# Delta rule in a hybrid decoder step: two rooms for the inverse W, and squares written over tiles that are filled next

## The chip, the cores and the metric

The kernel runs on one core of a Trainium2 chip. The metric is device time of one execution in microseconds, median of several runs. A core has five engines with queues of their own: TensorE (PE, with its weight loads as PEld), VectorE (DVE), ScalarE (ACT), GpSimd (POOL) and SyncE (SP, which here only issues transfers). Each engine takes its own queue in order; between engines, semaphores order the work.

## What is computed

One layer of a decoder trunk on 1024 prompt rows and 8 sample rows of width 1024: a projection, a gated delta rule (8 heads of 128 x 128), sliding-window attention, a gated mix, and a convolutional feed-forward block. The change touches the delta rule on the prompt alone. In the reference:

```python
u = jnp.einsum('bhnij,bhnjv->bhniv', t_inv, v * beta[..., None])
w = jnp.einsum('bhnij,bhnjk->bhnik', t_inv, kb * jnp.exp(decay)[..., None])
...
def step(S, inp):
    u_n, w_n, a_n, qd_n, kd_n, last_n = inp
    v_new = u_n - jnp.einsum('bhck,bhkv->bhcv', w_n, S)
    o = jnp.einsum('bhck,bhkv->bhcv', qd_n, S) + jnp.einsum('bhij,bhjv->bhiv', a_n, v_new)
    S = S * last_n[..., None, None] + jnp.einsum('bhck,bhcv->bhkv', kd_n, v_new)
    return S, o
```

`t_inv` is the inverse of a unit triangular matrix per chunk; `q` and `k` are divided by their row norms, and the output `o` of each row by its root mean square.

## The kernel before

The kernel works in chunks of 128 rows, 8 chunks a head. Around the change, five streams run for each head h (loop at L1889):

- **prepare** (`delta_prepare`, for head h+1): loads the decay row into G (L854), masks it on POOL (L855), subtracts on DVE (L857), exponentiates on ACT (L858). It turns K and Q chunk by chunk on PE (tile `tp`), sums their squares on ACT (L870, the squares themselves go to a junk tile `osq`), makes `kd` on DVE (L872), then the products K K and K Q on PE (L888, L889), from which DVE makes A (L890) and U (L892, in the room of G). V is turned into `vn` (L900).
- **inverse** (`unit_inverse`, head h): inverts the triangular blocks U. 15 steps of a recurrence on DVE (L1001, L1002), round trips through DRAM (`ud`, `wd`), and then three doublings: PE products L1020 and L1026 (32 x 32 blocks), L1038 and L1043 (32 x 32 off the diagonal), L1052 and L1056 (64 x 64). Results go from PSUM into W by ACT: the four diagonal blocks (L1031), the off-diagonal 32 blocks (L1047), the last 64 x 64 block (L1057). L1045 copies a block to the tile `w01`, which DVE turns (L1049) for L1052; L1053 copies the product of L1052 for L1056.
- **scan** (`delta_scan`, head h): the chain over 8 chunks. For each chunk: PE L929 (K with the state S), DVE L930 (y), PE L932 (W with y), ACT L934 (s), PE L936 (kd with s), DVE L945 (new S); beside it PE L939 and L940 sum the output. After chunks 3 and 7 ACT squares the four outputs (L951, squares to a junk tile `osq2`, which shares its name `osq` in the profile), DVE and POOL make the factor f, DVE scales into `vn` (L958), and PE turns that (L189, `rc<-ident,vn`).
- **gate** (head h) and **projections** (K, Q, V of head h+2, or later gates): long rows of matmuls at L180 to L182, out of `mm3`. They depend on nothing in the chain. I call them projections below; they are what PE does while it waits for the chain.

No order is written by hand. Streams carry priorities (`weave`: start and step in the list at L1894 to L1904), and a scheduler sets each engine's queue before the run, from the priorities, from what each instruction needs, and from the rooms: a tile with `bufs=1` can only be written once all readers of its last user are done. W is one tile for all heads (L1884), so L1031 of head h stands behind the last L932 of head h-1. The scheduler's order is fixed when the program runs.

Of the kernel before, what the change touches and what calls it, by code (L numbers as in the profile page):

```python
# [12 lines left out]
AF = mybir.ActivationFunctionType  # L13
# [5 lines left out]
P = 128  # L19
# [5 lines left out]
NCH = 8  # L25
# [39 lines left out]
class Step:  # L65
# [782 lines left out]
    def delta_prepare(self, pool, psum, h):  # L848
        nc = self.nc
        K, Q, V = self.kqv[h]  # L850

        G = self.t(pool, [P, NCH, P], "G", bufs=1)
        rows = self.drow[h * NCH:(h + 1) * NCH]
        nc.sync.dma_start(G, rows[:, 0, :].unsqueeze(0).broadcast_to([P, NCH, P]))  # L854
        nc.gpsimd.affine_select(out=G, in_=G, pattern=[[0, NCH], [1, P]], compare_op=ALU.is_ge, fill=NEG,  # L855
                                base=0, channel_multiplier=-1)
        nc.vector.tensor_tensor(G, G, bc(self.d[:, h, :], 2, P), op=ALU.subtract)  # L857
        nc.scalar.activation(G, G, AF.Exp)  # L858


        kd = self.t(pool, [P, NCH, P], "kd", bufs=2)
        n2 = self.t(pool, [P, 2, NCH], "n2", bufs=2)
        for a, src in ((0, K), (1, Q)):
            for c0 in (0, 4):
                tp = self.t(psum, [P, 4, P], "tp", bufs=2)
                for c in range(4):
                    self.transpose(tp[:, c, :], src[:, c0 + c, :])
                junk = self.t(pool, [P, P], "osq", bufs=1)
                for c in range(4):
                    nc.scalar.activation(junk, tp[:, c, :], AF.Square, accum_out=n2[:, a, c0 + c:c0 + c + 1])  # L870
                if a == 0:
                    nc.vector.tensor_tensor(kd[:, c0:c0 + 4, :], tp, bc(self.edd[:, h, c0:c0 + 4], 2, P), op=ALU.mult)  # L872
                yield
        nc.vector.tensor_scalar_add(n2, n2, 4 * EPS)
        nk = self.t(pool, [P, NCH], "nk", bufs=2)
        self.power(nk, n2[:, 0, :], self.phalf)
        nc.vector.tensor_scalar_mul(nk, nk, 0.5)
        c1 = self.t(pool, [P, 2, NCH], "c1", bufs=2)
        nc.vector.reciprocal(c1[:, 1, :], n2[:, 0, :])
        nc.vector.tensor_tensor(c1[:, 0, :], c1[:, 1, :], self.beta[:, h, 0:8], op=ALU.mult)  # L880
        nc.vector.tensor_scalar_mul(c1[:, 1, :], c1[:, 0, :], -1.0)

        A = self.t(pool, [P, NCH, P], "A", bufs=2)
        U = G
        for c0 in range(0, NCH, 2):
            kk = self.t(psum, [P, 2, 2, P], "tp", bufs=2)
            for c in range(2):
                nc.tensor.matmul(kk[:, 0, c, :], K[:, c0 + c, :], K[:, c0 + c, :], start=True, stop=True)  # L888
                nc.tensor.matmul(kk[:, 1, c, :], K[:, c0 + c, :], Q[:, c0 + c, :], start=True, stop=True)  # L889
            nc.vector.tensor_tensor(A[:, c0:c0 + 2, :], kk[:, 1], G[:, c0:c0 + 2, :], op=ALU.mult)  # L890
            for c in range(2):
                nc.vector.scalar_tensor_tensor(U[:, c0 + c, :], kk[:, 0, c, :], c1[:, 1, c0 + c:c0 + c + 1],  # L892
                                               G[:, c0 + c, :], op0=ALU.mult, op1=ALU.mult)
            yield
        vn = self.t(pool, [P, NCH, P], "vn", bufs=2)
        for c0 in (0, 4):
            tp = self.t(psum, [P, 4, P], "tp", bufs=2)
            for c in range(4):
                self.transpose(tp[:, c, :], V[:, c0 + c, :])
            nc.vector.tensor_tensor(vn[:, c0:c0 + 4, :], tp, bc(nk[:, c0:c0 + 4], 2, P), op=ALU.mult)  # L900
            yield
        for c in (0, 4):
            e = self.t(pool, [P, 4, P], "ed", bufs=1)
            nc.sync.dma_start(e, rows[c:c + 4, 1, :].unsqueeze(0).broadcast_to([P, 4, P]))
            nc.vector.tensor_tensor(Q[:, c:c + 4, :], Q[:, c:c + 4, :], e, op=ALU.mult)
        self.prep = U, kd, A, vn, n2, c1

    def delta_scan(self, pool, psum, h, prep):
        nc, sg = self.nc, self.sg
        (K, Qd, _), W = self.kqv[h], self.W  # L910
        _, kd, A, vn, n2, c1 = prep
        S = None
        self.steps, self.at, self.every = [], 0, 2

        def step(ins):
            if h + 2 >= H:
                self.steps.append(ins.ins)

        so = self.t(pool, [P, NCH], "so", bufs=2)
        f = self.t(pool, [P, NCH], "f", bufs=2)  # L920
        for n in range(NCH):
            if n % 4 == 0:
                ops = self.t(psum, [P, 4, P], "o", bufs=1)
            if S is None:
                y = vn[:, n, :]
            else:
                y = self.t(pool, [P, P], "y", bufs=2)
                ks = self.t(psum, [P, P], "rc", bufs=2)
                yield step(nc.tensor.matmul(ks, K[:, n, :], S, start=True, stop=True))  # L929
                nc.vector.scalar_tensor_tensor(y, ks, self.ned[:, h, n:n + 1], vn[:, n, :], op0=ALU.mult, op1=ALU.add)  # L930
            sp = self.t(psum, [P, P], "rc", bufs=2)
            yield step(nc.tensor.matmul(sp, W[:, n, :], y, start=True, stop=True))  # L932
            s = self.t(pool, [P, P], "s", bufs=2)
            nc.scalar.activation(s, sp, AF.Copy, scale=c1[:, 0, n:n + 1])  # L934
            ds = self.t(psum, [P, P], "rc", bufs=2)
            yield step(nc.tensor.matmul(ds, kd[:, n, :], s, start=True, stop=True))  # L936
            o = ops[:, n % 4, :]
            if S is not None:
                nc.tensor.matmul(o, Qd[:, n, :], S, start=True, stop=False)  # L939
            nc.tensor.matmul(o, A[:, n, :], s, start=S is None, stop=True)  # L940
            S2 = self.t(pool, [P, P], "S", bufs=2)
            if S is None:
                nc.vector.tensor_copy(S2, ds)
            else:
                nc.vector.scalar_tensor_tensor(S2, S, self.edl[:, h, n:n + 1], ds, op0=ALU.mult, op1=ALU.add)  # L945
            S = S2
            if n % 4 == 3:
                c0 = n - 3
                junk = self.t(pool, [P, P], "osq2", bufs=1)
                for c in range(4):  # L950
                    nc.scalar.activation(junk, ops[:, c, :], AF.Square, accum_out=so[:, c0 + c:c0 + c + 1])  # L951

                nc.vector.tensor_scalar_mul(so[:, c0:c0 + 4], so[:, c0:c0 + 4], 1.0 / P)
                nc.vector.scalar_tensor_tensor(so[:, c0:c0 + 4], n2[:, 1, c0:c0 + 4], EPS * P, so[:, c0:c0 + 4],
                                               op0=ALU.mult, op1=ALU.add)
                self.power(f[:, c0:c0 + 4], so[:, c0:c0 + 4], self.mhalf)
                on = vn[:, c0:c0 + 4, :]
                nc.vector.tensor_tensor(on, ops, bc(f[:, c0:c0 + 4], 2, P), op=ALU.mult)  # L958
            if n in (5, NCH - 1):
                c0 = 4 if n == NCH - 1 else 0  # L960
                tp = self.t(psum, [P, 4, P], "rc", bufs=2)
                for c in range(4):
                    self.transpose(tp[:, c, :], vn[:, c0 + c, :])
                g = sg[:, c0 * P:(c0 + 4) * P]
                nc.vector.scalar_tensor_tensor(g, tp.rearrange("p c i -> p (c i)"), self.onw, g,
                                               op0=ALU.mult, op1=ALU.mult)

        queue = nc.sync if h + 1 < H else nc.gpsimd
        queue.dma_start(self.O[2][0, 0, h], S)
        queue.dma_start(self.oa[h][:, 0:NP], sg[:, 0:NP])  # L970

    def unit_inverse(self, pool, psum, h, U):

        nc, W = self.nc, self.W
        ud = self.t(self.dr, [NCH, 4, 32, 32], "ud", bufs=2)
        blocks = [slice(32 * b, 32 * b + 32) for b in range(4)]
        pairs = [(blocks[0], blocks[1]), (blocks[2], blocks[3])]
# [4 lines left out]
        for p in range(4):  # L982
            c = slice(16 * (p % 2), 16 * (p % 2) + 16)
# [57 lines left out]
        for n in range(NCH):  # L1041
            for a, b in pairs:
                nc.tensor.matmul(qp[a, n, :], Zc[b, n, :], W32[b, n, :], start=True, stop=True)  # L1043
        w01 = self.t(pool, [32, NCH, 32], "w01", bufs=1)
        nc.scalar.copy(w01, qp[0:32])  # L1045
        for a, b in pairs:
            nc.scalar.copy(W[a, :, b], qp[a])  # L1047
# [784 lines left out]
    def run(self):  # L1832
        S, nc = ExitStack, self.nc
        self.constants()
        with S() as ca:
# [45 lines left out]
            self.fill_where, self.gt = [self.fill_side], (pgt, "gt")  # L1881
            with S() as c:
                pa, pool, psum = self.pool("pa", 1, ctx=c), self.pool("p4", 1, ctx=c), self.pool("q4", 1, PSUM, ctx=c)
                self.W = self.t(pool, [P, NCH, P], "W", bufs=1)  # L1884
                nc.gpsimd.memset(self.W, 0.0)
                self.kqv = {}
                self.weave((self.delta_project(pa, pool, 0), 0, 1))
                self.weave((self.delta_prepare(pool, psum, 0), 0, 1), (self.delta_project(pa, pool, 1), 100, 1))
# [66 lines left out]
```

## Time and profile before

| | us |
|---|---|
| runs | 2159.11, 2160.53, 2164.14 |
| median | 2160.53 |
| the profiled execution's own time | 2164.56 |
| its span, first to last instruction | 2162.7 |
| PE busy | 2087.4 |
| DVE busy | 1334.1 |
| ACT busy | 815.5 |
| POOL busy | 314.2 |
| mean granted TensorE clock (share of full) | 0.977 |

The delta rule's heads run from about 430 to 1140 us of the span. A row of the timeline gives start, length, engine, line, tiles and count; in brackets, how long the engine had been idle before it and who ended that. A row of the windows gives for a stretch the busy time of each engine, then the granted clock (PEclk). A matmul's length includes the depth of the array, so two matmuls in a row start closer together than their lengths say; the distance of starts is what a matmul costs. A plain f32 matmul is two rows of the profile, so one L932 counts as x2.

### The profile page before, as it was taken

The numbers are of one execution on the slowest core, as the hardware profiler recorded it, in microseconds if no ns is written. First come the engines' busy times: TensorE is split into PE (matmuls) and PEld (weight loads), VectorE is DVE, ScalarE is ACT, GpSimd is POOL, SyncE is SP. The second block draws the span as 40 slices with busy tenths as digits, with TensorE's granted clock in tenths as the row PEclk, the third lists the DMA queues.
The fourth block names the chain that finished last, engine by engine and source line by source line (L and its number), as shares of the span: only waits on it lengthen the run. The fifth ranks groups of instructions, "written<-read, shape, count | busy, mean of one in ns | idle before, by whom it ended". The sixth has DMA issues, their size and how long they took to land.

```text
span 2162.7 us, 41246 instructions
## 1 busy us (share of the span) xinstructions
PE 2087.4 (97%) x16514; PEld 1975.9 (91%) x16514; DVE 1334.1 (62%) x2884; ACT 815.5 (38%) x2093; POOL 314.2 (15%) x434
## 2 busy tenths in 40 slices
PE   7999999999899999998999999999999999999998
PEld 4876877899899998998999999999999999999998
DVE  6656775474564765665324665478867767865565
ACT  5544554333334344334222532354434334421102
POOL 3000000120321111111111100003323323100000
PEclk9999998999999989999999999999999999999999
DMA  9434231241322222221328845323232232353202
GB/s 330 141 101 160 82 121 43 82 128 38 88 65 74 60 67 58 47 67 49 89 62 253 288 128 147 114 64 99 79 99 69 69 98 69 114 218 124 75 3 80
DMA packets 257946, 223.91 MB, mean 104 GB/s; under 512 B 57586, under 2 KB 224277, under 8 KB 257738
## 3 DMA queue, kind: packets, MB, share of 16 engines
q1 hardware_dynamic: 254714, 212.50, 32.1%
q0 software_dynamic: 1568, 4.95, 0.7%
q10 hardware_dynamic: 1472, 3.82, 0.5%
q8 instruction: 130, 2.13, 0.4%
q14 instruction: 62, 0.51, 0.1%
HBM read 171.25 MB, written 52.33 MB: 103 GB/s over the span
## 4 chain that ended last, share of the span: by engine, by line
PE 61%; DVE 5%; DMA 3%; ACT 2%; issue 1%; POOL 1%; SPq 1%; POOLq 0%; DVEq 0%; ACTq 0%
PE mm L180 14%; PE mm L181 14%; PE mm L182 14%; PE wv L181 3%; PE wv L180 3%; PE wv L182 3%; PE wy L182 2%; PE wy L180 2%; PE wy L181 2%; DMA b1l<-dlr 1%; PE tp L189 1%; DVE fa L1629 1%; DMA raw<-in_w_o_dram 1%; PE rc L932 1%; PE rc L936 1%
## 5 line engine op out<-in xcount | busy, mean ns | idle before, releaser
L180 PE MATMUL mm<-b1h,wh 128*128 128x384 f32 (+1 forms) x1440 | 472.8, 330 | 5.2 <-ACT gt L1265 1.9
L181 PE MATMUL mm<-b1l,wh 128*128 128x384 f32 (+1 forms) x1440 | 467.5, 325 | 0.9 <-DVE b1l L130 0.9
L182 PE MATMUL mm<-b1h,wl 128*128 128x384 f32 (+1 forms) x1440 | 467.7, 326 | 0.6 <-DVE wl L130 0.5
L180 PEld LDWEIGHTS mm<-b1h,wh 128*128 128x128 f32 x1440 | 273.0, 190 | 13.3 <-issue 4.7
L181 PEld LDWEIGHTS mm<-b1l,wh 128*128 128x128 f32 x1440 | 273.6, 190 | 5.7 <-issue 4.1
L182 PEld LDWEIGHTS mm<-b1h,wl 128*128 128x128 f32 x1440 | 272.9, 190 | 6.4 <-issue 4.3
L130 DVE TENSOR_TENSOR wl<-raw,wh 128x1024 fp32r<-128x1024 f32 x76 | 92.9, 1222 | 69.4 <-ACT wh L129 68.4
L129 ACT ACTIVATE wh<-raw 128x1024 fp32r<-128x1024 f32 x77 | 80.6, 1047 | 124.2 <-PE mm L181 89.6
L180 PE MATMUL mm<-pk,w 128*128 128x260 f32 (+1 forms) x440 | 124.4, 283 | 1.0 <-ACT pk L129 0.6
L181 PE MATMUL mm<-pk,w 128*128 128x260 f32 (+1 forms) x440 | 124.2, 282 | 0.8 <-DVE pk L130 0.8
L182 PE MATMUL mm<-pk,w 128*128 128x260 f32 (+1 forms) x440 | 124.1, 282 | 0.0
L180 PE MATMUL mm<-b2h,wh 128*128 128x384 f32 (+1 forms) x384 | 122.8, 320 | 1.2 <-ACT wh L129 1.2
L181 PE MATMUL mm<-b2l,wh 128*128 128x384 f32 (+1 forms) x384 | 121.9, 318 | 0.0
L182 PE MATMUL mm<-b2h,wl 128*128 128x384 f32 (+1 forms) x384 | 121.3, 318 | 0.0
L180 PE MATMUL mm<-bmh,pk 128*128 128x260 f32 (+1 forms) x380 | 109.4, 288 | 1.9 <-ACT pk L129 1.8
L182 PE MATMUL mm<-bmh,pk 128*128 128x256 f32 (+1 forms) x380 | 109.5, 288 | 1.1 <-DVE pk L130 1.1
L1418 DVE SCALAR_TENSOR_TENSOR x<-mm,mT,x 128x256 f32<-128x256 f32 (+2 forms) x133 | 63.6, 482 | 74.7 <-PE mm L182 70.8
L181 PE MATMUL mm<-bml,pk 128*128 128x260 f32 (+1 forms) x353 | 101.1, 286 | 0.0
L180 PE MATMUL mm<-bmh,w 128*128 128x260 f32 (+1 forms) x320 | 91.0, 284 | 0.0
L182 PE MATMUL mm<-bmh,w 128*128 128x260 f32 (+1 forms) x320 | 90.8, 284 | 0.0
L130 DVE TENSOR_TENSOR w<-ws,w 128x512 fp32r<-128x512 f32 x88 | 60.2, 686 | 41.5 <-ACT w L129 41.5
L180 PEld LDWEIGHTS mm<-pk,w 128*128 128x128 f32 x440 | 82.7, 188 | 1.6 <-ACT pk L129 0.8
(607 smaller groups left out, 5708.2 us busy)
## 6 DMA issues: line engine op xcount, KB each, us to landing
raw<-in_w_in_dram SPq DMA_DIRECT2D x60, 512.0 KB
bml<-act SPq DMA_DIRECT2D x22, 516.0 KB
raw<-in_w_ffn_gate_dram SPq DMA_DIRECT2D x22, 512.0 KB
raw<-in_w_ffn_up_dram SPq DMA_DIRECT2D x22, 512.0 KB
raw<-in_w_ffn_down_dram SPq DMA_DIRECT2D x22, 512.0 KB
qst<-in_w_mod_dram SPq DMA_DIRECT2D x16, 512.0 KB
raw<-in_w_mod_dram SPq DMA_DIRECT2D x16, 512.0 KB
act<-fa SPq DMA_DIRECT2D x22, 260.0 KB
```

What stands on the lines that cost most here:

```text
L129: self.nc.scalar.activation(hi, x, AF.Copy)
L130: (eng or self.nc.vector).tensor_tensor(lo, x, hi.bitcast(F32), op=ALU.subtract)
L180: mm(ps, whi, xhi, start=first, stop=False, **kw)
L181: mm(ps, whi, xlo, start=False, stop=False, **kw)
L182: self.last = mm(ps, wlo, xhi, start=False, stop=last, **kw)
L189: return self.nc.tensor.transpose(out, in_, self.ident[:p, :p])
L932: yield step(nc.tensor.matmul(sp, W[:, n, :], y, start=True, stop=True))
L936: yield step(nc.tensor.matmul(ds, kd[:, n, :], s, start=True, stop=True))
L1418: nc.vector.scalar_tensor_tensor(x[:, :np_], ps[:, :np_], self.mT[:, m + j, 8:9], x[:, :np_], op0=ALU.mult, op1=ALU.add)
L1629: nc.vector.scalar_tensor_tensor(ai[:, c:e], zi[:, j + c:j + e], col(j), ai[:, c:e], op0=ALU.mult, op1=ALU.add)
```

## The change

- W becomes a list of two tiles, and head h uses `W[h % 2]`. Both are cleared once at the start.
- The tile A of a head is taken before the squares, and L870 writes the squares of K, then of Q, into A, chunk by chunk; L890 overwrites them later. The tile `osq` is gone.
- L951 writes the squares of the outputs into `vn`, which L958 overwrites next. The tile `osq2` is gone.
- L1045 copies into the first 32 partitions of U16, whose last reader L1020 is done by then. The tile `w01` is gone.

```diff
         kd = self.t(pool, [P, NCH, P], "kd", bufs=2)
         n2 = self.t(pool, [P, 2, NCH], "n2", bufs=2)
+        A = self.t(pool, [P, NCH, P], "A", bufs=2)
...
-                junk = self.t(pool, [P, P], "osq", bufs=1)
                 for c in range(4):
-                    nc.scalar.activation(junk, tp[:, c, :], AF.Square, accum_out=n2[:, a, c0 + c:c0 + c + 1])
+                    nc.scalar.activation(A[:, c0 + c, :], tp[:, c, :], AF.Square, accum_out=n2[:, a, c0 + c:c0 + c + 1])
...
-        A = self.t(pool, [P, NCH, P], "A", bufs=2)
...
-        (K, Qd, _), W = self.kqv[h], self.W
+        (K, Qd, _), W = self.kqv[h], self.W[h % 2]
...
-                junk = self.t(pool, [P, P], "osq2", bufs=1)
                 for c in range(4):
-                    nc.scalar.activation(junk, ops[:, c, :], AF.Square, accum_out=so[:, c0 + c:c0 + c + 1])
+                    nc.scalar.activation(vn[:, c0 + c, :], ops[:, c, :], AF.Square, accum_out=so[:, c0 + c:c0 + c + 1])
...
-        nc, W = self.nc, self.W
+        nc, W = self.nc, self.W[h % 2]
...
-        w01 = self.t(pool, [32, NCH, 32], "w01", bufs=1)
+        w01 = U16[0:32]
...
-                self.W = self.t(pool, [P, NCH, P], "W", bufs=1)
-                nc.gpsimd.memset(self.W, 0.0)
+                self.W = [self.t(pool, [P, NCH, P], f"W{i}", bufs=1) for i in range(2)]
+                for w in self.W:
+                    nc.gpsimd.memset(w, 0.0)
```

The scheduler lays the queues out anew from here, between 430 and 1230 us of the span; outside of that the order on PE is the same. No instruction is added but one POOL memset. After the change the line numbers are lower by one from L884 on and by two from L950 on (so L932 reads L931 there, and L1031 reads L1029). The text keeps the numbers of before.

**ACT, the end of head 4's inverse.** `z` and `th` belong to the projections and the gate, `s` to the scan of head 3, `tmp`, `w`, `W` and `UZ` to the inverse of head 4, `osq` is the junk tile. Before:

```order
L934 ACTIVATE s_8037<-rc_8035,c_1219_7568 128x128
L840 ACTIVATE th_8845<-mm_8820 128x384
L1040 COPY tmp_8724<-tp_8723 32x256 x2
L1045 COPY w_1411_8760<-tp_8725 32x256
L934 ACTIVATE s_8051<-rc_8049,c_1219_7568 128x128
L1031 COPY W_4385<-T_8640 32x8x32 x4
L1047 COPY W_4385<-tp_8725 32x8x32 x2
L951 ACTIVATE osq_1324_8059,so_7933<-o_7996 128x128
L1053 COPY UZ_8583<-tp_8765 64x512
```

After, at the same place:

```order
L1029 COPY W_723_4385<-T_8610 32x8x32 x4
L933 ACTIVATE s_8012<-rc_8010,c_1196_7546 128x128
L1038 COPY tmp_8694<-tp_8693 32x256 x2
L840 ACTIVATE th_8814<-mm_8789 128x384
L1043 COPY U_1354_8551<-tp_8695 32x256
L1045 COPY W_723_4385<-tp_8695 32x8x32 x2
L933 ACTIVATE s_8026<-rc_8024,c_1196_7546 128x128
L1051 COPY UZ_8553<-tp_8734 64x512
L949 ACTIVATE vn_7582,so_7909<-o_7971 128x128 x4
```

The four diagonal copies (L1031, here L1029) stood behind the scan's last L934, between it and L1053; now they stand ahead of the scan's last L934 but one. One square of the outputs stood ahead of L1053; now all four stand behind it.

**PE, the end of head 3's inverse.** `rc` and `o` belong to the scan of head 2, `tp` to the inverse (or, with `ident`, to the turning of K for head 4), `mm` to a projection. Before:

```order
L1043 MATMUL tp_7781<-T_7696,tmp_7780 32x32 x14
L929 MATMUL rc_7102<-S_7099,K_5244 128x128
L939 MATMUL o_7052<-S_7099,Q_5245 128x128
L1043 MATMUL tp_7781<-T_7696,tmp_7780 32x32 x2
L932 MATMUL rc_7105<-y_7101,W_4385 128x128
L1052 MATMUL tp_7821<-MR_7701,UZ_7639 64x64 x8
L936 MATMUL rc_7109<-s_7107,kd_6576 128x128
L940 MATMUL o_7052<-s_7107,A_6628 128x128
L1056 MATMUL tp_7831<-W_4385,UZ_7639 64x64 x8
L189 MATMUL tp_8466<-ident,K_7132 128x128 x4
```

After:

```order
L931 MATMUL rc_7087<-y_7083,W_723_4385 128x128
L180 MATMUL mm_10276<-b1h_111_485,wh_10214 128x264
L181 MATMUL mm_10276<-b1l_112_486,wh_10214 128x264
L182 MATMUL mm_10276<-b1h_111_485,wl_10215 128x264
L180 MATMUL mm_10276<-b1h_111_485,wh_10214 128x264
L181 MATMUL mm_10276<-b1l_112_486,wh_10214 128x264
L182 MATMUL mm_10276<-b1h_111_485,wl_10215 128x264
L1050 MATMUL tp_7797<-MR_7678,UZ_7616 64x64 x8
L935 MATMUL rc_7091<-s_7089,kd_6564 128x128
L939 MATMUL o_7034<-s_7089,A_6566 128x128
L1054 MATMUL tp_7807<-W_724_4386,UZ_7616 64x64 x8
L189 MATMUL tp_8441<-ident,K_7113 128x128 x4
```

Six projections have come between the scan's last L932 and L1052, and ahead of that L932 stand 18 more, behind L1043. Before, none stood from the scan's last L936 but two (ahead of L1026) to the second half of the products L888 and L889 for head 4.

**DVE, in the recurrence of head 1's inverse.** G is the decay mask of head 2, S and y belong to the scan of head 0, T and tmp to the recurrence. Before:

```order
L945 SCALAR_TENSOR_TENSOR S_5153<-S_5139,d_2416,rc_5149 128x128
L1002 TENSOR_REDUCE T_5747<-tmp_5771 128x8
L857 TENSOR_TENSOR G_6569<-G_6569,d_2414 128x1024
L1001 TENSOR_TENSOR tmp_5774<-T_5747,MR_5741 128x8x7
L953 TENSOR_SCALAR so_5101<-so_5101 128x4
```

After:

```order
L857 TENSOR_TENSOR G_6557<-G_6557,d_2414 128x1024
L999 TENSOR_TENSOR tmp_5762<-T_5738,MR_5732 128x8x6
L1000 TENSOR_REDUCE T_5738<-tmp_5762 128x8
L999 TENSOR_TENSOR tmp_5765<-T_5738,MR_5732 128x8x7
L1000 TENSOR_REDUCE T_5738<-tmp_5765 128x8
L999 TENSOR_TENSOR tmp_5768<-T_5738,MR_5732 128x8x8
L1000 TENSOR_REDUCE T_5738<-tmp_5768 128x8
L999 TENSOR_TENSOR tmp_5771<-T_5738,MR_5732 128x8x9
L1000 TENSOR_REDUCE T_5738<-tmp_5771 128x8
L999 TENSOR_TENSOR tmp_5774<-T_5738,MR_5732 128x8x10
L944 SCALAR_TENSOR_TENSOR S_5150<-S_5136,d_2416,rc_5146 128x128
```

L857 stood behind this S update and ahead of the next y; now it stands ahead of the S update too, with nine steps of the recurrence between.

## The prediction

> **What bounds the kernel.** I read the page first, then the windows of the delta rule's heads, and the timelines of PE, ACT and DVE at the ends of the heads' inverses.
>
> ```profile
> PE 2087.4 (97%) x16514; PEld 1975.9 (91%) x16514; DVE 1334.1 (62%) x2884; ACT 815.5 (38%) x2093; POOL 314.2 (15%) x434
> 430.00:1140.00 710.00, 682.74 (x5949) 656.78 (x5948) 396.16 (x866) 260.71 (x770) 128.20 (x190) 0.97 0.27 72
> ```
>
> PE is busy all but everywhere. The queues change between 430 and 1230 us alone, so a gain must come from PE's lost time there: 710 - 683 = 27 us idle, and what runs slowly. The number of PE instructions stays, and where projections fill PE there is nothing to win. It loses where none stand. These are the four stretches without projections, at the ends of the inverses of heads 3 to 6 (first four rows; the column before the last two is the granted clock), and the times of half rate in them:
>
> ```profile
> 753.97:777.77 23.80, 22.02 (x238) 19.20 (x237) 10.54 (x24) 14.54 (x57) 2.79 (x4) 0.64 0.17 55
> 833.02:852.32 19.30, 16.50 (x166) 14.08 (x166) 6.73 (x17) 13.68 (x56) 1.70 (x3) 0.82 0.09 33
> 907.57:927.80 20.23, 17.75 (x166) 15.62 (x166) 6.62 (x16) 13.80 (x56) 1.55 (x3) 0.75 0.08 31
> 990.31:1004.94 14.63, 10.56 (x104) 9.39 (x102) 6.13 (x13) 11.22 (x44) 1.31 (x2) 0.77 0.24 78
> 759.27:776.34 17.07, 16.50 (x112) 14.33 (x111) 6.01 (x14) 12.08 (x53) 1.30 (x2) 0.50 0.15 54
> 841.19:848.02 6.83, 6.19 (x34) 5.39 (x34) 2.57 (x6) 5.20 (x25) 1.02 (x1) 0.50 0.00 0
> ```
>
> Their granted clocks say the same of the others: 0.75 over 20.23 us is 10.1 us of half rate, 0.77 over 14.63 is 6.7. So the four lose to idling (11 us) and to some 41 us at half rate. In the second, PE and ACT in order of time:
>
> ```profile
> 837.19 0.49 PE L932 MATMUL rc<-y,W 128*128 128x128 f32 x2
> 838.14 0.49 PE L936 MATMUL rc<-s,kd 128*128 128x128 f32 x2 [0.46 <-ACT s L934]
> ...
> 838.78 1.14 PE L1052 MATMUL tp<-MR,UZ 64*64 64x64 f32 x16
> 841.58 1.96 PE L1056 MATMUL tp<-W,UZ 64*64 64x64 f32 x16 [1.66 <-ACT UZ L1053]
> ...
> 848.66 0.60 PE L189 MATMUL tp<-ident,Q 128*128 128x128 f32 x4
> 849.09 0.39 PE L929 MATMUL rc<-S,K 128*128 128x128 f32 x2
> 849.32 0.39 PE L939 MATMUL o<-S,Q 128*128 128x128 f32 x2
> ```
>
> ```profile
> 837.72 0.37 ACT L934 ACTIVATE s<-rc,c 128x128 f32<-128x128 f32 x1
> 837.98 1.66 ACT L1031 COPY W<-T 32x256 f32<-32x256 f32 x4
> ...
> 840.95 0.58 ACT L1053 COPY UZ<-tp 64x512 f32<-64x512 f32 x1
> ...
> 843.58 0.58 ACT L1057 COPY W<-tp 64x512 f32<-64x512 f32 x1 [0.86 <-PE tp L1056]
> 844.63 0.28 ACT L870 ACTIVATE osq<-tp 128x128 f32<-128x128 f32 x1 [0.47 <-PE tp L189]
> ...
> 845.03 0.28 ACT L870 ACTIVATE osq<-tp 128x128 f32<-128x128 f32 x1
> ```
>
> L1052 ends at 839.9, but the copy for L1056 begins at 840.95: ahead of it in ACT's queue the four copies into W (1.66 us) had waited for the scan's last L932, the last reader of the one W. That is the wait which the second room takes away. Behind L1056 ACT sets the pace too: a square costs 0.40 us from start to start, sixteen of them 6.4.
>
> **The change, part by part.** Prices at full rate, as distances of starts: a pair (one L929, L939 and so on) 0.23 us (849.09 to 849.32), four turnings 0.43 (848.66 to 849.09), L1052 1.1.
>
> *In-place squares and `w01` in U16: nothing.* The same ACT and DVE instructions run with the same sizes; the outputs go to SBUF as before. New waits: L870 needs A's room free, whose last reader L940 stands right behind L936, the last reader of `kd`'s room, which the same step needs anyway; L951 overwrites `vn` rows that the y of the same chunks has read; U16's next writer comes one head later. If that cover goes, L870 waits one pair, 0.23. I take 0. The added POOL memset runs beside other work at the start; POOL is 15% busy.
>
> *Stretches, up to L1056.* The other three L1056, the longest idle time ahead of the fall of the clock in head 3 (757.27), and the price of 32 small matmuls (834.22 to 834.84):
>
> ```profile
> 757.27 0.49 PE L932 MATMUL rc<-y,W 128*128 128x128 f32 x2 [0.80 <-DVE y L930]
> 766.14 1.97 PE L1056 MATMUL tp<-W,UZ 64*64 64x64 f32 x16
> 834.22 0.69 PE L1038 MATMUL tp<-MR,U 32*32 32x32 f32 x32
> 834.84 0.49 PE L936 MATMUL rc<-s,kd 128*128 128x128 f32 x2
> 916.13 1.86 PE L1056 MATMUL tp<-W,UZ 64*64 64x64 f32 x16 [1.66 <-ACT UZ L1053]
> 996.67 1.96 PE L1056 MATMUL tp<-W,UZ 64*64 64x64 f32 x16 [0.67 <-ACT UZ L1053]
> ```
>
> Head 3 takes 766.14 - 753.97 = 12.2. Its own work: 12 pairs 2.8, a turning 0.4, L1026 at most 1.2 (64 matmuls at L1038's price of 0.62 for 32), L1038 and L1043 0.6 each, L1052 1.1: 6.7, so 5.5 are lost. In the new order projections stand between its links up to L1052. What stays is the copy L1053: with ACT's queue clear the row at 996.67 gives 0.67, and the pairs L936 and L940 now stand in it: 0.2 to 0.3. Saved 5.2. Head 6: 996.67 - 990.31 = 6.4, own work 2.4 (3 pairs, L1043, L1052), lost 4.0; projections come in there too, saved 3.7. Heads 4 and 5 get no projections: from the end of L1043 (about 837.2) to L1056 were 4.4 us. Now L929, L939, then a round trip over DVE of 0.95 (as L932 to L936, 837.19 to 838.14), L932, L1052 1.1, and the copy with two pairs in it, 0.7: with 0.4 for small waits 3.2. Saved 1.2 each; head 5 is given the same as head 4, since the idle time before its L1056 (1.66) and its counts (x166) are alike.
>
> *Stretches, from L1056 on.* Before: 777.77 - 766.14 = 11.6, 852.32 - 841.58 = 10.7, 927.80 - 916.13 = 11.7, 1004.94 - 996.67 = 8.3. After, by ACT's queue behind L1053: four output squares 1.6, L1057 0.6, sixteen squares 6.4, one L934 0.4, then PE's four last pairs and an L932, 1.1: 10.1. Saved 1.5, 0.6, 1.6; head 6 has eight more products (L888, L889) in its stretch than before, 1.8, so 0.
>
> *Half rate.* In head 3 half rate began at 759.27 with no idle time over 0.80 us ahead of it in the stretch, so shorter gaps don't end it: in the new stretches I let L1056 run at half rate (1.97 for 1.14) in all four heads, -3.2. Under the ACT pace the rest of it is hidden. The Trainium skill, page "TensorE: Matmul & The Clock Gate", section "Part 1: The HAM clock gate", has the clock fall only after a whole idle window of about 3.4 us. By that rule none of these stretches would have fallen, and the sum below would be 10.3 in place of 7.1; the trace disagrees (longest idle before the fall at 841.19: 1.66 us), and I go by it.
>
> *New waits.* In heads 1 and 2 L857 moves on DVE past the S update and the y of a scan. L857 waits for G's transfer and POOL's mask:
>
> ```profile
> 552.80 0.07 DVE L985 MEMSET MR<- 128x16 f32 x1 [0.17 <-DMA MR<-ud]
> 559.82 1.52 DVE L857 TENSOR_TENSOR G<-G,d 128x1024 f32<-128x1024 f32 x1 [2.87 <-POOL G L855]
> 561.79 0.27 DVE L1001 TENSOR_TENSOR tmp<-T,MR 128x64 f32<-128x64 f32 x1
> 562.09 0.22 DVE L1002 TENSOR_REDUCE T<-tmp 128x8 f32<-128x64 f32 x1
> 562.94 0.49 PE L932 MATMUL rc<-y,W 128*128 128x128 f32 x2 [3.40 <-DVE y L930]
> 640.12 1.23 DVE L857 TENSOR_TENSOR G<-G,d 128x1024 f32<-128x1024 f32 x1 [1.65 <-POOL G L855]
> 832.68 0.34 PE L182 MATMUL mm<-b1h,wl 128*128 128x384 f32 x1
> 832.85 0.34 PE L180 MATMUL mm<-b1h,wh 128*128 128x384 f32 x1
> ```
>
> Call X the start of L985; L857 can start at X+7.0. Head 1 after: between L985 and y stand a step over 1024 columns (1.23 like L857's) and one of the recurrence, so y is done by X+1.8; L932, 20 projections at 0.17, L936, 4 projections: L929 wants S at X+6.3. S stands behind L857 (X+8.3) and nine steps at 0.25: X+10.6. So 4.3 idle, and 0.8 on the next y, which now has no projection ahead of it: 5.1 in place of 3.4, about -2. Head 2: y stands behind L857, ready at X+9; 33 projections cover to X+7.4: -1.7, where before this wait (1.65 on DVE) cost PE nothing. The turning of `vn` in head 2 also comes closer behind the scan's last L940, with the output squares, f and L958 between: -1.
>
> **Sum.** Head 3 5.2 + 1.5, head 4 1.2 + 0.6, head 5 1.2 + 1.6, head 6 3.7: 15.0. Less 3.2 half rate, less 4.7 new waits: 7.1. The profiled execution, 2164.56, would come to 2157.5; it lies 4.0 above the median, from which I forecast: 2160.53 - 7 = **2153.5**. The later stages start earlier by as much.
>
> **Rivals.** (B) *The gain is eaten.* ACT's squares pace the stretches as before, and half rate stays throughout; head 3's projections gain 5.2 and head 6's half of 3.7, and the new waits take 4.7: 2158. For it: the x166 rows keep their whole work in heads 4 and 5. Against it: 1.66 us leave ACT's queue there. The Trainium skill, same page, section "Part 4: PE-mode transpose", states that turnings on PE don't count as work for the clock; the new order has eight turnings of K, four of `vn` and eight of Q almost in a row, so by that rule B comes true. Here the clock came back at 848.02 after some 3 us that were mostly turnings (848.66 is one at full rate), so the trace rather speaks against it.
>
> (C) *Slower: DVE stands behind G.* L857 now comes earlier in heads 1 to 6, mostly ahead of a scan's S or y. If G lands as late as in head 1 (X+7.0) in every head, each loses 4.3 as there; the wait decides once G is over 1 us later than the DVE instructions ahead of L857. Heads 1 to 5 then lose 4.3 x 5 = 21.5 in place of 3.4, against 15.0 - 3.2 gained: 2160.5 + 18.1 - 11.8 = 2167. Against it: projections cover 3 to 5 us in heads 3 on, and only heads 1 and 2 showed the wait reaching far.
>
> (D) *More.* Half rate goes from the stretches, and L857's new places fit: 15.0 with no deduction: 2145.5.
>
> **Chances.** Forecast 0.52 (own range 2149 to 2156), B 0.26, C 0.10, D 0.12. A measurement here tells 0.2% (4.3 us) from no change: forecast and D are faster, with a slice of B: faster 0.66; B's rest is the same: 0.24; C slower: 0.10. Range 2144 to 2163.
>
> **What would show it.** Right: L1031 in heads 3 to 6 starts before the scan's last L932; idle before L1056 there under 0.5; head 3's stretch shrinks from 23.8 to about 12, its half rate from 17 to under 10. PE idles some 4 us on S in head 1's recurrence. Wrong: stretches as long as before, idle time moved to `rc<-ident,vn` or to `kd`, half rate near 41 us again; or PE waiting for y and S in heads 3 to 6.

## The result and the profile after

The median after is 2144.89 us (2140.55 to 2146.0, 4 runs) beside 2161.41 (2159.11 to 2164.14, 4 runs): ratio 0.9919, 95% interval 0.9901 to 0.9938, 16.5 us faster. The direction was forecast, and the time lies in the wide range (2144 to 2163), but below the forecast's own (2149 to 2156): the size was forecast as 7. It is the time of the rival D, whose first half (half rate goes from the stretches) came true.

The after's lines are numbered as in its own code: L1054 is the L1056 of before, L1051 the L1053, L1029 the L1031, L931 the L932. First the page of the profile and the row of the delta rule's heads:

```profile
PE 2071.7 (97%) x16514; PEld 1959.6 (91%) x16514; DVE 1330.7 (62%) x2884; ACT 799.6 (37%) x2093; POOL 313.1 (15%) x435
430.00:1130.00 700.00, 677.61 (x6022) 651.42 (x6021) 404.41 (x881) 253.70 (x783) 129.05 (x192) 1.00 0.29 79
```

The granted clock is 1.00 where it was 0.97. PE runs the same 16514 instructions in 15.7 us less. The heads 3 to 6 can be compared exactly: from the L1056 of head 3 to that of head 6, PE runs the same work in both kernels. These two rows (before, then after; columns as before: length, busy time of PE, PEld, DVE, ACT, POOL, then the clock) carry the result:

```profile
766.14:996.67 230.53, 221.25 (x1981) 211.59 (x1980) 148.32 (x329) 92.40 (x281) 32.32 (x55) 0.94 0.23 59
```

```profile
762.55:978.04 215.49, 209.47 (x1980) 200.01 (x1981) 149.06 (x328) 83.70 (x274) 33.73 (x55) 1.00 0.25 63
```

15.0 us shorter. The two profiled executions lie 19.2 us apart (2164.56 and 2145.34); 3.6 of these are there by head 3's last doubling (766.14 and 762.55). Of the 15.0 PE's idle time gives 3.3 (230.53 - 221.25 = 9.3 before, 6.0 after) and PE's busy time 11.8: the same instructions at full rate. So in PE's account the gain is mostly the clock. That is not yet proof that the clock alone would bring it: below, getting it back by other means gains some 5 us at most.

Head 4's inverse, PE in order of time (beside the same place of before in the prediction):

```profile
830.96 0.49 PE L931 MATMUL rc<-y,W 128*128 128x128 f32 x2 [0.22 <-DVE y L929]
831.56 1.11 PE L1050 MATMUL tp<-MR,UZ 64*64 64x64 f32 x16
832.61 0.49 PE L935 MATMUL rc<-s,kd 128*128 128x128 f32 x2
832.93 0.39 PE L939 MATMUL o<-s,A 128*128 128x128 f32 x2
833.35 1.14 PE L1054 MATMUL tp<-W,UZ 64*64 64x64 f32 x16
834.42 1.39 PE L189 MATMUL tp<-ident,K 128*128 128x128 f32 x8
836.84 0.66 PE L189 MATMUL rc<-ident,vn 128*128 128x128 f32 x4 [1.03 <-DVE vn L956]
...
842.87 0.39 PE L180 MATMUL mm<-b1h,wh 128*128 128x264 f32 x1 [0.69 <-DVE sg L841]
```

And ACT there; the rows that read the squares' sums are left out:

```profile
824.77 1.67 ACT L1029 COPY W<-T 32x256 f32<-32x256 f32 x4
...
832.71 0.58 ACT L1051 COPY UZ<-tp 64x512 f32<-64x512 f32 x1 [0.86 <-PE tp L1050]
833.36 0.28 ACT L949 ACTIVATE vn<-o 128x128 f32<-128x128 f32 x1
...
834.52 0.58 ACT L1055 COPY W<-tp 64x512 f32<-64x512 f32 x1
835.11 0.28 ACT L870 ACTIVATE A<-tp 128x128 f32<-128x128 f32 x1
...
835.38 0.27 ACT L870 ACTIVATE A<-tp 128x128 f32<-128x128 f32 x1
835.63 0.28 ACT L870 ACTIVATE A<-tp 128x128 f32<-128x128 f32 x1
```

Two things are to be seen. The four diagonal copies are done 4.5 us before the scan's last L931 (824.77 + 1.67 = 826.44, and 830.96), ACT waits for L1050 and not the other way round, and PE's idle time ahead of the last doubling, 1.66 us, is 0.03. And a square costs 0.25 us from start to start, where it cost 0.40: before, all squares went to the one junk tile; now each has its own place in A. That the place makes the price is shown by the first experiment.

### The profile page after: what moved, and what is told of

Same layout as the page of the kernel before. It is cut to its first block, busy times and chain, and to the rows that moved or that the text cites. A ratio compares the mean times of both kernels' runs of the same rounds, so it can differ in the third digit from the quotient of the medians.

```text
span 2143.5 us, 41258 instructions
## 1 busy us (share of the span) xinstructions
PE 2071.7 (97%) x16514; PEld 1959.6 (91%) x16514; DVE 1330.7 (62%) x2884; ACT 799.6 (37%) x2093; POOL 313.1 (15%) x435
## 4 chain that ended last, share of the span: by engine, by line
PE 60%; DVE 6%; DMA 4%; issue 2%; ACT 2%; SPq 1%; POOL 0%; DVEq 0%; POOLq 0%; ACTq 0%
PE mm L180 14%; PE mm L181 13%; PE mm L182 13%; PE wv L181 3%; PE wv L180 3%; PE wv L182 3%; PE wy L182 2%; PE wy L180 2%; PE wy L181 2%; DMA b1l<-dlr 1%; DVE fa L1627 1%; DVE wl L130 1%; PE rc L931 1%; DMA raw<-in_w_o_dram 1%; PE rc L928 1%
## 5 line engine op out<-in xcount | busy, mean ns | idle before, releaser
L130 DVE TENSOR_TENSOR wl<-raw,wh 128x1024 fp32r<-128x1024 f32 x76 | 93.1, 1224 | 54.6 <-ACT wh L129 53.3
```

The lines of the kernel that those rows point to most:

```text
L130: (eng or self.nc.vector).tensor_tensor(lo, x, hi.bitcast(F32), op=ALU.subtract)
```

## The experiments

The rows below are all of the three distances from head 3's last doubling to head 6's (230.53 before, 215.49 after).

**One slot.** Two rooms for W without the fast squares. (The rooms were not tried beside the junk tiles and `w01`.)

```diff
-                    nc.scalar.activation(A[:, c0 + c, :], tp[:, c, :], AF.Square, ...)
+                    nc.scalar.activation(A[:, c0, :], tp[:, c, :], AF.Square, ...)
...
-                    nc.scalar.activation(vn[:, c0 + c, :], ops[:, c, :], AF.Square, ...)
+                    nc.scalar.activation(vn[:, c0, :], ops[:, c, :], AF.Square, ...)
```

> The kernel after, but the four squares of a group all go to one slot of A (or of vn), so each overwrites the one before, as with the junk tiles; the two rooms stay. Theory R (rooms; it is the prediction's): the address of a square costs nothing, so the time is that of after, 16 us under before (13 to 18). Theory S (squares): the distance of two squares goes back from 0.25 us to the 0.40 of before; a stretch at the end of an inverse holds 16 to 20 squares, so 2.4 to 3.0 us of ACT's pace come back in each of four heads, 10 to 12 us, and the time is only 4 to 7 us under before; half rate comes back in some of the stretches.

2153.92 us, ratio 0.9973 (0.9958 to 0.9988): 5.8 us under before. The squares are back at 0.40 (ACT, head 4), and half rate is back, 27.3 us of it at heads 3 to 6:

```profile
841.10 0.28 ACT L870 ACTIVATE A<-tp 128x128 f32<-128x128 f32 x1 [0.47 <-PE tp L189]
841.50 0.28 ACT L870 ACTIVATE A<-tp 128x128 f32<-128x128 f32 x1
```

```profile
764.58:988.27 223.69, 216.41 (x1980) 208.62 (x1980) 148.86 (x328) 89.07 (x275) 34.25 (x55) 0.95 0.24 61
837.39:844.22 6.83, 6.16 (x36) 5.73 (x37) 2.75 (x6) 4.18 (x19) 1.02 (x1) 0.50 0.10 41
```

R is wrong (13 to 18 forecast) and the time speaks for S. But the scheduler also laid the queues anew. PE's order in heads 4 and 5, from the second products (L1024) to the last doubling, with the number of projections as F, the scan's links by their lines, L939 and L938 left out:

```
after:     L1024 L928 L1024 F26 L931 F3 L1036 F2 L935 L1041 L928 L931 L1050 L935 L1054
one slot:  L1024 L931 L1024 L935 L928 L1036 L931 L1041 L935 L1050 L1054
```

So nothing tells yet whether the pace or the order matters.

**Squares alone**, one room.

```diff
-                self.W = [self.t(pool, [P, NCH, P], f"W{i}", bufs=1) for i in range(2)]
+                self.W = self.t(pool, [P, NCH, P], "W", bufs=1)
```

> The kernel before with the squares in A and vn and the block copy in U16, but with one room for W. Theory R: no gain, 0 to 3 us either way, since the four diagonal copies still stand between the scan's last s and the copy that the last doubling waits for, and half rate stays near 41 us. Theory S: squares at 0.25 us, 10 to 12 us faster, and most of the half rate gone. If both parts are needed to keep the clock up, neither alone gives much: 3 to 6 us here.

2158.82 us, ratio 0.9993 (0.9983 to 1.0003): no change that can be told, clock 0.94 in its row. Slow squares with two rooms give 5.8 us, fast squares with one room 1.5, both 16.5: the parts don't add up, and both R and S are too simple.

```profile
759.21:985.45 226.24, 217.58 (x1980) 210.86 (x1981) 149.55 (x329) 83.97 (x274) 34.60 (x56) 0.94 0.24 62
```

**A junk tile of four slots.**

```diff
-                junk = self.t(pool, [P, P], "osq", bufs=1)
+                junk = self.t(pool, [P, 4, P], "osq", bufs=1)
...
-                junk = self.t(pool, [P, P], "osq2", bufs=1)
+                junk = self.t(pool, [P, 4, P], "osq", bufs=1)
...
-                    nc.scalar.activation(junk, ops[:, c, :], AF.Square, ...)
+                    nc.scalar.activation(junk[:, c, :], ops[:, c, :], AF.Square, ...)
```

> The kernel before with a junk tile of four slots, one for each square of a group; nothing is written in place, one room for W. Theory S: what counts is that a square doesn't overwrite the one before, so squares run at 0.25 us inside a group of four, one at 0.40 between groups, and the time is that of the squares alone less one or two us: 8 to 11 us faster. Theory R: as before within 3 us.

2331.7 us, ratio 1.0795 (1.0777 to 1.0814): 170 us slower, and all theories missed. For the sake of space both squares got tiles of one name, where before has two (`osq`, `osq2`). ACT around the end of head 3's scan:

```profile
896.33 0.28 ACT L951 ACTIVATE osq<-o 128x128 f32<-128x128 f32 x1
896.74 0.28 ACT L870 ACTIVATE osq<-tp 128x128 f32<-128x128 f32 x1
897.01 0.27 ACT L870 ACTIVATE osq<-tp 128x128 f32<-128x128 f32 x1
```

The first L870 of head 4's prepare follows 0.4 us behind the last L951 of head 3's scan, and so in every head looked at (580.9 and 581.6, 693.9 and 694.4, 796.6 and 797.0); in before head 4's squares began at 769.2, 73 us ahead of that L951. So prepare of head h+1 now stands behind the scan of head h, which fits rooms of one name being handed on in the order of the source; a kernel with four slots under two names was not run. The pace was 0.25, as S has it, but this run says nothing else on S.

**`w01` alone.**

```diff
-        w01 = self.t(pool, [32, NCH, 32], "w01", bufs=1)
+        w01 = U16[0:32]
```

> The kernel before with the block copy in U16 alone: no wait and no pace changes by any theory, but the scheduler lays its queues anew. R and S: within 0.2% (4.3 us) of before. If a new layout by itself moves the time (theory L), 5 us or more either way.

2162.48 us, ratio 1.0003 (0.9990 to 1.0015). As all but L expected; this part did nothing for the time but make space.

**Turnings that keep PE at work.** Since half rate went and came in these runs, the next four kernels add useless full-size work where PE waits.

```diff
         zp = self.t(psum, [P, NCH, 2, 32], "tp", bufs=2)
+        for _ in range(6):
+            self.transpose(zp[:, 0:2].rearrange("p n a i -> p (n a i)"), self.ident)
...
-        qp = self.t(psum, [64, NCH, 64], "tp", bufs=2)
+        qp = self.t(psum, [P, NCH, 64], "tp", bufs=2)
+        for _ in range(6):
+            self.transpose(qp[:, 0:2].rearrange("p n i -> p (n i)"), self.ident)
+        qp = qp[0:64]
```

With one slot:

> The kernel with two rooms and slow squares, and six more turnings of a 128 x 128 constant on PE ahead of L1052 and six ahead of L1056 (overwritten by these). In the runs so far a window of 3.41 us is followed by half rate where its full-size matmuls, turnings among them, plus half of its 64-row ones fill under some 43% of it; 32-row ones hardly count. Theory G (the gate counts such work, and half rate is what the slow squares cost): the 27 us of half rate at heads 3 to 6 fall under 10, and the time falls by 4 to 8 us to 2146 to 2150, although PE does 1.3 us a head more. Theory P (ACT's pace is the bound, and half rate is hidden under it): half rate falls too, but the time stays at 2154 or rises by up to 5. Theory I (the gate follows idle time alone, turnings don't count): half rate stays at 27 us or more.

2150.81 us, ratio 0.9949 (0.9932 to 0.9966). Half rate left heads 3 to 6 wholly, and 96 turnings more made the kernel some 5 us faster than the one-slot one (0.9973), though the ends of the two intervals overlap. In the row, PE is busy for 216.1 us with 36 turnings more, against 216.4, and the distance is 1.8 us shorter:

```profile
763.61:985.48 221.87, 216.11 (x2018) 204.95 (x2017) 147.97 (x330) 90.09 (x280) 32.59 (x57) 1.00 0.25 62
```

G's half rate came, and I is wrong; G's time (2146 to 2150) is missed by 0.8 us. The order changed here too, so that the turnings did it is not yet shown. In the kernels after, before, and with squares alone:

> The same twelve turnings a head in the kernel after, where heads 3 to 6 hold no half rate: their price alone. 12 x 0.107 us = 1.3 us a head, 10 us over eight heads if nothing hides them, 2 if PE's waits do. All theories: 2 to 10 us slower than after, 2147 to 2155, half rate in the delta stage still under 10 us.

> The same turnings in the kernel before. G: its 41 us of half rate at heads 3 to 6 fall under 15 and the time by 5 to 10 us, to 2151 to 2156, as half rate was a cost of its own. P: half rate falls, the time does not (2160 to 2166). I: half rate stays near 41.

> The same turnings with the fast squares and one room, which alone gained 1.5 us and kept 34 us of half rate at heads 3 to 6. G: half rate falls under 10 us and the time to 2147 to 2153: then the second room's share in the gain is the clock. P: no more than 2 us below 2159: then it is the four diagonal copies ahead of L1051 on ACT. I: half rate stays.

After: 2157.0 us, ratio 0.9982 (0.9969 to 0.9995), some 13 us slower than without, more than the 10 that the turnings cost when nothing hides them; half rate in the delta stage rose from 6.8 to 13.7 us with the new order (its profile is of its fastest run, 2151.37). Before: 2164.9, ratio 1.0012 (1.0001 to 1.0023): half rate fell from 47.8 to 20.5 us, but the time rose, so G misses. From head 3's last doubling to head 6's this kernel takes 228.06 us for 230.53, but it reaches head 3's 4.3 us later (770.46 for 766.14): the turnings cost elsewhere what they gained there. Squares alone: 2155.16, ratio 0.9968 (0.9955 to 0.9981), some 5 us faster, and half rate from 41.0 to 17.1; between G and P. As far as these four go, whose orders changed as well, useless work pays where it lies in waits at half rate and costs its price elsewhere, and getting the clock back this way gains some 5 us at most, net of the turnings' price.

**Small products in place of the turnings.** Sixteen 32 x 32 products at each place were to take as long on PE as the six turnings:

```diff
-        for _ in range(6):
-            self.transpose(zp[:, 0:2].rearrange("p n a i -> p (n a i)"), self.ident)
+        for _ in range(16):
+            nc.tensor.matmul(zp[0:32, 0, 0], self.ident[0:32, 0:32], self.ident[0:32, 0:32], ...)
```

(and the same into `qp`.)

> The kernel with one slot, and in place of the six turnings sixteen more 32 x 32 products ahead of L1052 and sixteen ahead of L1056, about as long on PE (0.62 us a place against 0.64). Theory G (full-size work counts for the clock, 32-row work hardly does): unlike with the turnings, half rate stays: 10 us or more at heads 3 and 4, where no projections stand behind L1043, and 15 us or more at heads 3 to 6 together; the time no better than the one-slot kernel's 2154, up to 2162. Theory B (any busy time counts): half rate under 7 us at heads 3 to 6 as with the turnings, and 2148 to 2153.

2180.14 us, ratio 1.0076 (1.0055 to 1.0096). Half rate is as G has it, 44.4 us at heads 3 to 6; the time is 18 us above G's range. The products cost more than the estimate: at full rate the last head's sixteen take 1.12 us up to the L1059 behind them (at 1098.99), its six turnings in the other kernel 0.81 (L1059 at 1072.89):

```profile
1097.87 1.19 PE L1056 MATMUL tp<-ident 32*32 32x32 f32 x32
```

```profile
1072.08 0.88 PE L189 MATMUL tp<-ident 128*128 128x128 f32 x6
```

Against the turnings it is 27 us slower, with work that keeps PE busy longer, not shorter. Not all of the 27 us is the clock: the products' price is part of it, and the order is another here too (in head 5 no projection stands between the first products of the inverse and its last doubling). First the three distances; then three windows of the clock's grid of 3.41 us in head 4:

```profile
774.20:1011.17 236.97, 231.47 (x2174) 222.26 (x2172) 146.59 (x325) 87.62 (x271) 33.65 (x54) 0.92 0.22 54
841.36:844.77 3.41, 2.55 (x67) 2.00 (x67) 1.55 (x5) 3.08 (x10) 0.00 (x0) 1.00 0.03 7
844.77:848.18 3.41, 3.20 (x62) 3.09 (x57) 1.43 (x4) 1.97 (x9) 1.30 (x2) 0.50 0.06 19
848.18:851.60 3.42, 3.42 (x41) 2.91 (x40) 0.58 (x2) 0.58 (x1) 0.00 (x0) 0.50 0.00 0
```

What PE ran in the last of them (L1052 and L1059 are the two last doublings in this kernel, L1056 the added products):

```profile
846.94 1.94 PE L1052 MATMUL tp<-MR,UZ 64*64 64x64 f32 x16 [0.21 <-DVE MR L1047]
848.81 1.16 PE L1056 MATMUL tp<-ident 32*32 32x32 f32 x18
849.90 1.11 PE L189 MATMUL rc<-ident,vn 128*128 128x128 f32 x4
850.94 0.95 PE L1056 MATMUL tp<-ident 32*32 32x32 f32 x14
851.83 1.97 PE L1059 MATMUL tp<-W,UZ 64*64 64x64 f32 x16
```

The window 848.18 to 851.60 is busy from end to end, and the next is granted half rate all the same (L1059 takes 1.97). But it ran at half rate itself, where the same work fills more time. The clean comparison is with the first of the three, which ran at full rate and was busy for 75%, and half rate followed. Put beside it a window of the kernel after, in its head 4, also at full rate and busy for 67%, which kept the full clock in the next one (the eight turnings, the vn's four and some of Q's lie in it):

```profile
834.55:837.96 3.41, 2.29 (x18) 1.78 (x18) 2.18 (x6) 2.87 (x18) 1.02 (x1) 1.00 0.03 7
```

So in these heads it isn't idle time alone that the clock follows; full-size work keeps it where small products don't. How far that goes is said at the end.

**The order apart from the squares.** A step of the streams' list (how the projections' priorities grow) changes no work, but gives heads 5 and 6 of the kernel after the order that they have with one slot, up to the last doubling, and the other way round.

```diff
-                               (self.head_projections(pa, pool, h), 600, 100)]
+                               (self.head_projections(pa, pool, h), 600, 70)]
```

In the kernel after, and in the one with one slot:

> The kernel after with the projections' step in the list of streams at 70 in place of 100: no work changes, but the scheduler gives heads 5 and 6 the order of PE up to L1054 that they have in the kernel with one slot (no projection between the first products and L1054 in head 5, two groups in head 6), with fast squares. Theory O (order: where no projections stand between the inverse's links, the windows hold too little full-size work, and half rate follows; the squares' pace matters only through the order that the scheduler lays): half rate of 3.4 to 7 us at each of heads 5 and 6, none or little at 3, and the two distances of L1054 around head 5 (71.4 and 73.3 in after) grow by 2 to 3 us each, to those of the one-slot kernel (73.5 and 76.8); the time 2147 to 2153. Theory S (squares' pace itself): no half rate at heads 5 and 6, distances as in after, 2143 to 2147.

> The kernel with slow squares (one slot) with that step at 70: heads 5 and 6 get, up to L1054, the order of PE that they have in the kernel after (26, 3 and 2 projections between the links of head 5), with slow squares. O: no half rate at heads 5 and 6 but for 3.4 us at most, and the distances around head 5 near 72 and 74; the time 3 to 8 us under the one-slot kernel's 2154. S: half rate of 6.8 us at both, distances 73.5 and 76.8, the time as with one slot, 2152 to 2156.

After with 70: 2155.4 us, ratio 0.9963 (0.9947 to 0.9979): some 9 of the 16.5 us are gone with nothing but the order, more than O expected. One slot with 70: 2153.54, ratio 0.9964 (0.9946 to 0.9982), no faster as a whole than with 100; O's time is missed; heads 3 and 4 got 6.8 and 10.2 us of half rate in their new order. The heads 5 and 6 answer the question:

| distance to head 5 / 6 (us), half rate there (us) | order of after | order of one slot |
|---|---|---|
| squares at 0.25 | 71.4 / 73.3, 0 and 0 | 73.3 / 76.2, 10.2 and 6.8 |
| squares at 0.40 | 72.0 / 74.8, 3.4 and 3.4 | 73.5 / 76.8, 6.8 and 6.8 |

The order is worth 1.5 to 2.9 us a head, the squares' pace within one order 0.2 to 1.5. (Up to the last doubling the orders of a column are the same on PE; behind it they still differ a little, so the second figure holds some of that too.) PE after with step 70, in head 5: squares at 0.25, and half rate from 904.85 on, where the longest gap in the window ahead is 0.22 us; what stood there were links of the inverse and the scan with no projection:

```profile
901.96 0.49 PE L928 MATMUL rc<-S,K 128*128 128x128 f32 x2 [0.22 <-DVE S L944]
902.28 0.39 PE L938 MATMUL o<-S,Q 128*128 128x128 f32 x2
902.60 0.69 PE L1036 MATMUL tp<-MR,U 32*32 32x32 f32 x32
903.22 0.49 PE L931 MATMUL rc<-y,W 128*128 128x128 f32 x2
903.81 1.08 PE L1041 MATMUL tp<-T,tmp 32*32 32x32 f32 x32
904.81 0.79 PE L935 MATMUL rc<-s,kd 128*128 128x128 f32 x2
```

A second order for the kernel after, and one for the kernel before:

```diff
-                               (self.head_projections(pa, pool, h), 600, 100)]
+                               (self.head_projections(pa, pool, h), 500, 100)]
```

> The kernel after with the projections' start at 500 in place of 600: head 3 keeps its projections between the links, heads 4 and 5 have none there and head 6 nineteen in place of 55; fast squares, two rooms. O: half rate of 3.4 to 7 us at each of heads 4, 5 and 6, together 10 to 20 us, none at head 3; the distances of L1054 from head 3 to 6 (70.8, 71.4, 73.3 in after) grow by 2 to 3 us each; the time 2148 to 2155. S: as after, 2143 to 2147.

> The kernel before, nothing of the change, with the projections' step at 50: 28, 28 and 50 projections stand between the links of heads 4 to 6 in place of 24, 24 and 31, but behind the last of them the round trips L1043, L1052, L1056 stay bare, one room, slow squares. O: 5 to 10 us of the 41 us of half rate go, 2 to 6 us faster than before. If the room and the squares are needed for their own sake: within 0.2% of before.

After with start 500: 2156.83 us, ratio 0.9976 (0.9963 to 0.9989); half rate of 6.8 us at each of heads 4, 5 and 6, none at head 3, as O has it, and slower than its 2148 to 2155.

```profile
760.36:985.55 225.19, 215.09 (x1981) 205.96 (x1981) 151.72 (x332) 85.02 (x283) 39.86 (x57) 0.97 0.25 63
```

Before with step 50: 2166.14, ratio 1.0019 (1.0006 to 1.0033), slightly slower and with more half rate (54.6 us): O misses. More projections ahead of the links don't help where the last round trips stay bare, and I have no kernel of before with the order of after.

**After once more.**

> The kernel after once more, beside the kernel before on the same chip as the run above. If its full clock comes from its order: 14 to 19 us under before again, half rate at heads 3 to 6 under 7 us. If the first profile only happened to fall well against the grid of the clock's windows: 8 to 13 us, and half rate of 10 us or more at heads 3 to 6.

2143.77 us, ratio 0.9908 (0.9888 to 0.9928), some 20 us under before where 14 to 19 were expected, no half rate at all in the delta stage, and the same three distances:

```profile
760.63:975.76 215.13, 209.12 (x1980) 199.97 (x1980) 148.82 (x328) 83.85 (x274) 33.78 (x55) 1.00 0.25 63
```

## Why the prediction had the direction right and the size wrong

**What bounds the kernel.** Right. The four stretches without projections, their idle time and half rate, were what the gain came out of.

**The diagonal copies.** Right: they moved ahead of the scan's end, and the idle time before the last doubling is 0.19, 0.03, 0.03 and 0 us in heads 3 to 6 (under 0.5 forecast). Head 3's stretch fell from 23.8 to 10.8 us (760.57 to 771.35; about 12 forecast).

**Half rate, -3.2.** This step failed first. I let L1056 run at half rate in all four heads, as a deduction, because half rate in before began with no gap over 0.80 us ahead of it. That gaps don't decide was read rightly (though of the 1.66 us named for the fall at 841.19 only 1.27 lie ahead of it, L1056 began at 841.58); the conclusion was wrong. By the experiments what ran between the gaps counts, and the new order has projections and turnings there. L1054 took 1.14 us in all four. The one-slot kernel keeps half rate and gains 5.8 us, where 7.1 was the sum; that is near by luck, as its order is not the one that the sum was made for.

**New waits, -4.7.** Failed too. L857 does wait as forecast (the row names z, but POOL's mask L855 ended just then, at 556.50), and S does come late: X is 549.34, L857 starts at X+7.2 (X+7.0 forecast), S at X+11.1 (X+10.6 forecast). The DVE rows:

```profile
549.34 0.07 DVE L983 MEMSET MR<- 128x16 f32 x1
...
556.53 1.56 DVE L857 TENSOR_TENSOR G<-G,d 128x1024 f32<-128x1024 f32 x1 [2.36 <-POOL z L789]
...
560.42 0.34 DVE L944 SCALAR_TENSOR_TENSOR S<-S,d,rc 128x128 f32<-128x128 f32 x1
```

But by then PE had lost 2.5 us on another wait, for ACT to empty a room of the projections, which the prediction does not have; so it reached L928 only 0.83 us early, where some 4 were forecast. PE there, and then its waits from 430 to 1130 us (us in total, times, longest):

```profile
556.33 0.39 PE L180 MATMUL mm<-b1h,wh 128*128 128x264 f32 x1 [2.54 <-ACT gt L1263]
560.81 0.49 PE L928 MATMUL rc<-S,K 128*128 128x128 f32 x2 [0.83 <-DVE S L944]
```

```profile
PE rc L189 <- DVE vn L956: 5.1, 5, 1.1
PE mm L180 <- ACT gt L1263: 3.1, 3, 2.5
PE rc L931 <- DVE y L929: 2.4, 5, 1.2
PE rc L928 <- DVE S L944: 2.3, 3, 1.0
```

What PE lost on ACT it no longer lost on S: the two waits overlap. From head 0's L1056 to head 1's PE idled 6.8 us before and 7.1 after, and from there to head 2's 2.2 and 0 (the work there is not quite the same in both). So the 4.7 us did not come.

The first row was a sign that the prediction gave for being wrong: idle time moved to `rc<-ident,vn`. It came, 1.0 to 1.1 us in each of heads 3 to 6 and 0.9 in head 2, where the whole delta stage of before has this:

```profile
PE rc L189 <- DVE vn L958: 1.2, 2, 0.9
```

It cost these 4 us and the stretches got shorter all the same; -1 for it was forecast in head 2 alone.

**From L1056 on, "in-place squares: nothing".** Mis-sized. I took 0.40 us a square as the price of a square; 0.15 of it was the price of the one slot (0.25 after). With ACT's pace at 0.40 I had 10.1 us from L1056 to the first projection. Measured: 8.8, 9.5, 8.7 and 8.7, so 2.8, 1.2, 3.0 and -0.4 saved (6.6) where 3.7 stood. How much of the 2.9 us between is the pace itself is not shown: in the one-slot kernel, with squares at 0.40 but another order, the same four take 8.4, 8.2, 9.4 and 9.2. The table above limits the direct worth of the pace too; the rest would have to act through the order and the clock.

**The sum.** Both deductions taken out, the sum is the 15.0 of rival D; measured 16.5. That it comes so near is partly luck. From head 3's L1056 to head 6's its terms are 6.1 up to L1056 (1.2 + 1.2 + 3.7) and 3.7 behind it (1.5 + 0.6 + 1.6), 9.8 in all; measured in the profiles are 15.0, of which 8.0 up to L1056 and 7.0 behind it. Up to head 3's L1056 it has 5.2, and 3.6 came. B and C did not come: half rate left, and no wait of PE for y or S is longer than 1.2 us. On the clock, the Trainium skill ("TensorE: Matmul & The Clock Gate", "Part 1: The HAM clock gate") has it fall after an idle window of about 3.4 us; the emptiest window ahead of a fall was busy for 24%, the fullest for 88%, in 68 falls of fifteen profiles. Its "Part 4: PE-mode transpose" has turnings not count as busy time in the same way; windows that were mostly turnings kept the full clock (834.55 above). The measurement decides in both.

What stays open: why each part alone moves the scheduler to a poorer order. That another order alone takes some 9 to 11 of the 16.5 us away is shown; that these belong to the two parts, and not to a lucky fall of the scheduler, is not: two neighbouring settings lose them. Nor is shown how much of an order's worth is its clock and how much its waits: no kernel here has the whole order of after at half rate.

## What to carry to other kernels

Where a tensor engine fills its waits with small products, look at how much full-size work each few microseconds hold, not at the gaps alone. Full-size work in a wait can cost less than the clock that it keeps (some 5 us gained here in two kernels), but it cost 13 us, with the order that came with it, where the clock was full already. A result that nobody reads still has a place, and writing it to one slot again and again cost 0.15 us a square here; and a name shared by two streams can tie them together. Where a scheduler sets the order, an edit's gain is that of the order which it happens to get: move one neutral setting and time it again before you put the gain down to the edit.

## What the runs showed of the chip

- The clock is granted in windows of 3.413 us on a fixed grid, whose place differs between executions (whether that is why runs of one kernel differ by some us is not shown). In fifteen profiles (all but that of the four slots) the 2,964 windows at full rate between 430 and 1130 us can be sorted by one number: the share of full-size matmul time, turnings among it, plus half of the 64-row and a quarter of the 32-row time. Under 0.47 half rate followed in 50 of 50, above it in 18 of 2,914; the window ahead of 904.85 above is one of these 18, at 0.54. Sorted by plain busy time, the best cut puts 45 wrong; with turnings counted as nothing, the best cut is hardly better than none (67 wrong, 68 without a cut). With the run of the four slots it is 23 wrong of 3,114 for the number and 48 for busy time.
- The weights are a fit to these windows, no more. In the rest of the program, where products of other shapes run, the same number is no better than plain busy time (77 and 70 wrong in 5,918 windows with 130 falls). So it is shown for this stretch alone, not as a rule of the clock.
- At half rate the eight 64-row products of a doubling took 1.97 us for 1.14, and four turnings 0.86 (919.68 to 920.54 in before) for 0.43.
- A square on ACT costs 0.25 us from start to start into its own place, 0.40 into the place of the one before it (835.38 to 835.63 in after, 841.10 to 841.50 with one slot).
